# One product for the recurrence's diagonal and its lowest level

## The chip, the cores and the metric

The kernel runs on one core of a Trainium2 chip. The metric is the device time of one execution in microseconds, as the median of several runs. TensorE multiplies matrices and writes PSUM, VectorE (DVE in the profile) and ScalarE (ACT) work element by element, GpSimd (POOL) fills and copies in SBUF, and SyncE (SP) issues the loads.

## The reference, cut to what matters

The program is a two-layer trunk over 256 tokens of width 1024. Each layer is a half SwiGLU, a mixer, and another half SwiGLU. The change is in the mixer of layer 0, a gated linear recurrence (HGRN2) with 6 heads of dimension 128, beside a memory attention:

```
f = lb + (1 - lb) * sigmoid(f_raw);  q = silu(q_raw);  k = 1 - f;  v = i_raw
S_t = diag(f_t) S_{t-1} + k_t v_t^T        # per head, S is 128 x 128
o_t = S_t^T q_t
main = rms_norm(o, hgrn_o_gain) * silu(g_raw)
```

Written as scores, `o_t = sum over s <= t of (q_t * f_{s+1} ... f_t * k_s) v_s`. The score of a token with itself is `q_t . k_t`, the diagonal.

## The kernel before, in words

All data has features on the 128 partitions and tokens along the free dimension. The dense products (projections, SwiGLU) stream their weights in pieces of 128x1024 through SBUF. Each piece is split into two fp32r parts, `wh` by a cast on ScalarE (L367) and `wl` by a subtraction on VectorE (L368), and each product is taken as three fp32r matmuls.

The recurrence is computed as scores between tokens, by levels. For a block size m of 64, 32, 16, 8, 4, 2 and 1 (`LEVELS`), the tokens lie in pairs of neighbouring blocks of m. A level covers the scores of the upper block's queries with the lower block's keys. Heads go in three pairs (`hg` = 0, 1, 2), so a pair of heads has 4 tiles of 128 tokens by 128 tokens (j = 0 to 3).

`running(hg)` prepares the operands from the lowest level up. For each level, ScalarE copies the lower blocks' k into a slot of a "hid" tile (L971) and VectorE writes f times q for the upper blocks beside it (L972). Two further VectorE operations carry the running products of f to the next level, in place in `ks` and `f` (L976, L979).

`scores(hg)` does the products, in fp32. First comes the diagonal: 4 products of k with q, of 128 columns each, into one "lb" bank of PSUM, which VectorE multiplies by the identity into the score tile `s` (L1000). Then the levels come in pairs, 64/32, 16/8, 4/2, and 1 alone. Each has 4 products of 64 moving columns (the queries of the upper blocks), and a masked copy puts each level into `s` (L1017, `copy_predicated`). At last the cross product between the two tiles of each head is taken, two products, copied by ScalarE (L1024). After each bank the function pauses for a time of the planner (`DELAY["s0"]` and so on, 0.72 to 0.8 us), and dense matmuls stand in between.

The order on TensorE is fixed by a planner, `Flow`: chains such as `recurrence`, `hgrn_out`, `mem_attention` and `normed_T` are generators with due times, and after each three dense matmuls `flow.tick()` lets one due chain go on. The planner's clock runs by a cost per matmul (in `mm`) and the pauses in `DELAY`. Other engines' instructions are put in order by the framework.

Buffers that matter: "lb" has 2 PSUM banks, "mm" 3, "tb" 2, "ob" 1. "b6" has 8 SBUF buffers of 128x1560; in this mixer they hold f, kT, q, ks, i, g and a passing sq. "hid" has 11. A wait of the planner, `has("b6")`, holds a chunk until a buffer is free. The diff's `free("b6", 5)` returns the recurrence's buffers.

The mixer's projections run as chunks in the order "MMfqfqmfqigigig" (f, q, i and g of the recurrence; m and M of the memory attention), with the recurrence's products between them.

Of the kernel before, what the change touches and what calls it, by code (L numbers as in the profile page):

```python
# [15 lines left out]
ALU = mybir.AluOpType  # L16
AX = mybir.AxisListType

P = 128
T = 256  # L20
# [7 lines left out]
LEVELS = (64, 32, 16, 8, 4, 2, 1)  # L28
# [209 lines left out]
def trunk(ctx: ExitStack, tc: tile.TileContext, d: dict, out: bass.AP):  # L238
    nc = tc.nc
    V, S, G = nc.vector, nc.scalar, nc.gpsimd  # L240
# [11 lines left out]
    def bank(tag):  # L252
        return ps.tile([P, 512], F32, tag=tag, name=tag, bufs=room[tag])

    def take(tag):
        assert live[tag] < room[tag], tag
        live[tag] += 1

    def free(tag, n=1):
        live[tag] -= n  # L260
        freed[tag] = flow.now
# [7 lines left out]
    def hid():  # L269
        take("hid")  # L270
        return sb.tile([P, 4 * T], F32, tag="hid", name="hid", bufs=room["hid"])

    def b6(dt=F32):
        take("b6")
        return sb.tile([P, 1560], dt, tag="b6", name="b6", bufs=room["b6"])
# [4 lines left out]
    def unit():  # L280
        return sb.tile([P, 6 * P], F32, tag="unit", name="unit", bufs=3)
# [5 lines left out]
    def split_tiles():  # L287
        h = sb.tile([P, KT, T], F32R, tag="xh", name="xh", bufs=2)
        l = sb.tile([P, KT, T], F32R, tag="xl", name="xl", bufs=2)
        return h, l  # L290


    def mm(out, lhsT, rhs, start, stop):
        n = int(np.prod(rhs.shape[1:]))
        passes = 4 if rhs.dtype == F32 or n < 256 else 1
        flow.now += max(passes * n / 2400, 0.054) + 0.002
        nc.tensor.matmul(out=out, lhsT=lhsT, rhs=rhs, start=start, stop=stop, skip_group_check=True)  # L297
# [61 lines left out]
    def parts():  # L359
        wh = sb.tile([P, PIECE], F32R, tag="wh", name="wh", bufs=NBUF)  # L360
        wl = sb.tile([P, PIECE], F32R, tag="wl", name="wl", bufs=NBUF)
        ready.append((wh, wl))
        return wh, wl
# [16 lines left out]
    def take_piece():  # L380
        used[0] += 1
        return ready.pop(0)
# [49 lines left out]
    ident = sb.tile([P, P], F32, tag="ident", name="ident")  # L432
# [400 lines left out]
    x = split_tiles()  # L833
# [23 lines left out]
    for i in range(4):  # L857
        w = take_piece()
# [4 lines left out]
        w = parts()  # L863
# [13 lines left out]
    masks = sb.tile([P, len(LEVELS), 64], U8, tag="masks", name="masks")  # L877
# [52 lines left out]
    f, kT = b6(), b6()  # L930
# [18 lines left out]
    box = {}  # L949

    def slot(hg, i):

        return es[hg][i // 2][:, (i % 2) * 512:(i % 2 + 1) * 512]

    def halves(ap, m):
        v = ap.rearrange("p (n w m) -> p n w m", w=2, m=m)
        return v[:, :, 0, :], v[:, :, 1, :]

    def running(hg):


        es[hg] = [hid() for _ in range(4)]
        sl = slice(hg * 512, (hg + 1) * 512)
        fp, ks, k, q = f[:, sl], box["ks"][:, sl], kT[:, sl], qT[:, sl]
        for i in reversed(range(len(LEVELS))):
            m = LEVELS[i]
            n = 256 // m
            src = k if m == 1 else ks
            (f0, f1), (s0, s1) = halves(fp, m), halves(src, m)
            e0, e1 = halves(slot(hg, i), m)  # L970
            S.copy(out=e0, in_=s0)  # L971
            V.tensor_tensor(out=e1, in0=f1, in1=halves(q, m)[1], op=ALU.mult)  # L972
            low, up = f0[:, :, m - 1:m].broadcast_to([P, n, m]), f1[:, :, m - 1:m].broadcast_to([P, n, m])
            if m < 64:
                k0, k1 = halves(ks, m)
                V.tensor_tensor(out=k0, in0=s0, in1=up, op=ALU.mult)  # L976
                if m == 1:
                    S.copy(out=k1, in_=s1)
                V.tensor_tensor(out=f1, in0=f1, in1=low, op=ALU.mult)  # L979
            else:  # L980

                x = slot(hg, 7).rearrange("p (h t w m) -> p h t w m", h=2, t=2, w=2)
                h4 = lambda ap: ap.rearrange("p (h t) m -> p h t m", h=2)
                f0, f1, s0, s1, e1, q0, q1 = map(h4, (f0, f1, s0, s1, e1, *halves(q, m)))
                one = lambda ap, t: ap[:, :, t, 63:64].broadcast_to([P, 2, 64])
                V.tensor_tensor(out=x[:, :, 0, 0, :], in0=s0[:, :, 0, :], in1=one(f1, 0), op=ALU.mult)
                S.copy(out=x[:, :, 0, 1, :], in_=s1[:, :, 0, :])
                V.tensor_tensor(out=x[:, :, 1, 0, :], in0=f0[:, :, 1, :], in1=q0[:, :, 1, :], op=ALU.mult)
                V.tensor_tensor(out=x[:, :, 1, 1, :], in0=e1[:, :, 1, :], in1=one(f0, 1), op=ALU.mult)
            yield DELAY["lv"]  # L990

    def scores(hg):
        s = unit().rearrange("p (j c) -> p j c", j=6)
        ss[hg] = s
        b = bank("lb").rearrange("p (j c) -> p j c", j=4)
        for j in range(4):
            h, tt = 2 * hg + j // 2, j % 2
            sl = slice(h * T + tt * P, h * T + (tt + 1) * P)
            mm(b[:, j, :], kT[:, sl], qT[:, sl], j == 0, True)
        V.tensor_tensor(out=s[:, 0:4, :], in0=b, in1=ident.unsqueeze(1).broadcast_to([P, 4, P]), op=ALU.mult)  # L1000
        yield DELAY["s%d" % hg]
        for i0 in range(0, len(LEVELS), 2):
            b = bank("lb").rearrange("p (a j c) -> p a j c", a=2, j=4)
            pair = range(i0, min(i0 + 2, len(LEVELS)))
            for i in reversed(pair):
                m = LEVELS[i]
                for j in range(4):
                    e = slot(hg, i)[:, j * P:(j + 1) * P]
                    rows = P - m if m >= 16 else P
                    mm(b[0:rows, i - i0, j, :], e[:, 0:rows],  # L1010
                       e.rearrange("p (n w m) -> p n w m", w=2, m=m)[:, :, 1, :], i == pair[-1] and j == 0, True)
            for i in pair:
                m = LEVELS[i]
                rows = P - m if m >= 16 else P
                sv = s[0:rows, 0:4, :].rearrange("p j (n w m) -> p j n w m", w=2, m=m)[:, :, :, 1, :]
                mk = masks[0:rows, i, :].rearrange("p (n m) -> p n m", m=m)
                V.copy_predicated(out=sv, mask=mk.unsqueeze(1).broadcast_to([rows, 4, 64 // m, m]),  # L1017
                                  data=b[0:rows, i - i0].rearrange("p j (n m) -> p j n m", m=m))
            yield DELAY["s%d" % hg]
        b = bank("lb")  # L1020
        for hh in range(2):
            e = slot(hg, 7)[:, hh * T:(hh + 1) * T]
            mm(b[:, hh * P:(hh + 1) * P], e[:, 0:P], e[:, P:T], hh == 0, True)
        S.copy(out=s[:, 4:6, :], in_=b[:, 0:2 * P].rearrange("p (j c) -> p j c", j=2))  # L1024
        free("hid", 4)
        got["s"].add(hg)

    def recurrence(hg):
        yield lambda: hg in got["q"] and len(fc) > hg and fc[hg].done and (hg == 0 or hg - 1 in got["x"])
        yield lambda: live["hid"] + 4 <= room["hid"]  # L1030
        if hg == 0:
            take_ks()
        yield from running(hg)
        got["x"].add(hg)
        yield DELAY["x"]
        yield from scores(hg)
        if hg == 2:
            free("b6", 4)

    def take_ks():  # L1040
        box["ks"] = b6()

    def hgrn_out(hg):
        yield lambda: hg in got["s"] and hg in got["v"] and (hg == 2 or hg in got["g"])
# [40 lines left out]
    for hg in range(3):  # L1085
        flow.spawn(recurrence(hg), prio=PRIO["rec"])
    hc = [flow.spawn(hgrn_out(hg), prio=PRIO["hc"]) for hg in range(3)]
    mixed, mem_c, tiles = [], [], {}
    qT = None
# [243 lines left out]
```

## Time and profile before

| what | value |
|---|---|
| time before, median of 3 runs | 1061.81 us (1061.71 to 1062.89) |
| the profiled execution's own time | 1061.96 us |
| its span | 1060.2 us |
| TensorE busy | 1048.8 us (99%) |
| VectorE busy | 723.8 us (68%) |
| ScalarE busy | 533.7 us (50%) |
| GpSimd busy | 80.0 us (8%) |

The span is the time from the first to the last instruction. Busy shares are means over the whole program. Mixer A of layer 0, where the change lies, runs from about 205 to 345 us. PE is TensorE's matmuls, PEld its weight loads, which run beside them.

### The profile page before, as it was taken

How to read it: one execution, taken by the hardware profiler on the slowest of the kernel's cores; microseconds unless marked ns; L12 is line 12 of the kernel's file. 1: busy time of each engine (PE TensorE's matmuls, PEld its weight loads, DVE VectorE, ACT ScalarE, POOL GpSimd, SP SyncE). 2: the span in 40 equal slices, each digit the busy share in tenths (PEclk: the TensorE clock that was granted, in tenths of full speed). 3: DMA queues.
4: the chain of work that ended last, by engine and by line, in shares of the span. 5: the costliest groups of instructions: out<-in, count | busy, mean ns of one | idle time of the engine just before them, and what ended most of it. 6: DMA issues, size and time to landing. Idle time of an engine off the chain costs nothing.

```text
span 1060.2 us, 21472 instructions
## 1 busy us (share of the span) xinstructions
PE 1048.8 (99%) x8834; PEld 1042.8 (98%) x8834; DVE 723.8 (68%) x1331; ACT 533.7 (50%) x816; POOL 80.0 (8%) x107
## 2 busy tenths in 40 slices
PE   9899999999999999999999999999999999999998
PEld 9899999999999999999999999999999999999998
DVE  6866667689956776666687766666776577666652
ACT  7654545455544454444446544444477346445431
POOL 1000002110010500001110000012100040000000
PEclk9999999999999999999999999999999999999999
DMA  9566555553323465555553755555533245555561
GB/s 352 192 204 224 204 194 180 188 176 134 122 99 120 163 209 186 182 196 180 186 172 122 234 184 195 184 189 189 176 123 120 100 160 183 192 182 188 196 195 60
DMA packets 52874, 186.42 MB, mean 176 GB/s; under 512 B 6288, under 2 KB 7720, under 8 KB 52776
## 3 DMA queue, kind: packets, MB, share of 16 engines
q1 hardware_dynamic: 52776, 185.05, 51.3%
q8 instruction: 69, 1.13, 0.4%
q14 instruction: 29, 0.24, 0.1%
HBM read 183.95 MB, written 1.05 MB: 175 GB/s over the span
## 4 chain that ended last, share of the span: by engine, by line
PE 93%; DVE 3%; ACT 2%; DMA 2%; issue 0%; POOL 0%; SPq 0%; DVEq 0%; ACTq 0%
PE mm L297 63%; PE lb L297 26%; PE ob L297 2%; PE tb L301 1%; DMA xT<-in_xT 1%; DVE wl L368 1%; DMA b<-in_first 1%; PE tb L297 0%; ACT wh L367 0%; ACT hid L680 0%; POOL ss L481 0%; SPq L423 0%; ACT hid L487 0%; DVE small L451 0%; DVE small L453 0%
## 5 line engine op out<-in xcount | busy, mean ns | idle before, releaser
L368 DVE TENSOR_TENSOR wl<-raw,wh 128x1024 fp32r<-128x1024 f32 (+1 forms) x338 | 417.5, 1236 | 187.5 <-ACT wh L367 186.2
L367 ACT CAST wh<-raw 128x1024 fp32r<-128x1024 f32 (+1 forms) x338 | 350.8, 1039 | 297.3 <-PE mm L297 155.0
L297 PE MATMUL mm<-xh,wh 128*128 128x256 f32 x928 | 261.4, 282 | 0.0
L297 PE MATMUL mm<-xh,wl 128*128 128x256 f32 x928 | 259.1, 279 | 0.0
L297 PE MATMUL mm<-xl,wh 128*128 128x256 f32 x928 | 259.0, 279 | 0.0
L297 PE MATMUL mm<-hid,wh 128*128 128x256 f32 x1408 | 250.1, 281 | 0.0
L297 PEld LDWEIGHTS mm<-hid,wh 128*128 128x128 f32 x1408 | 216.0, 188 | 0.0
L297 PE MATMUL lb<-xh,wh 128*128 128x256 f32 x704 | 198.4, 282 | 1.6 <-ACT wh L367 1.6
L297 PE MATMUL lb<-xh,wl 128*128 128x256 f32 x704 | 197.4, 280 | 1.5 <-DVE wl L368 1.5
L297 PE MATMUL mm<-hid,wl 128*128 128x256 f32 x704 | 197.8, 281 | 0.0
L297 PE MATMUL lb<-xl,wh 128*128 128x256 f32 x704 | 197.2, 280 | 0.0
L297 PEld LDWEIGHTS mm<-xh,wh 128*128 128x128 f32 x928 | 174.5, 188 | 0.1
L297 PEld LDWEIGHTS mm<-xl,wh 128*128 128x128 f32 x928 | 174.5, 188 | 0.1
L297 PEld LDWEIGHTS mm<-xh,wl 128*128 128x128 f32 x928 | 174.4, 188 | 0.0
L297 PEld LDWEIGHTS lb<-xh,wh 128*128 128x128 f32 x704 | 133.0, 189 | 1.8 <-ACT wh L367 1.8
L297 PEld LDWEIGHTS lb<-xh,wl 128*128 128x128 f32 x704 | 133.0, 189 | 1.7 <-DVE wl L368 1.7
L297 PEld LDWEIGHTS lb<-xl,wh 128*128 128x128 f32 x704 | 133.2, 189 | 0.1
L297 PEld LDWEIGHTS mm<-hid,wl 128*128 128x128 f32 x704 | 132.6, 188 | 0.0
L297 PE MATMUL mm<-wh,xh 128*128 128x256 f32 x384 | 116.9, 304 | 0.0
L297 PE MATMUL mm<-wl,xh 128*128 128x256 f32 x384 | 108.2, 282 | 0.0
L297 PE MATMUL mm<-wh,xl 128*128 128x256 f32 x384 | 107.9, 281 | 0.0
L551 ACT CAST hid<-tmp 128x256 fp32r<-128x256 f32 x88 | 35.5, 406 | 93.9 <-DVE tmp L550 93.9
(177 smaller groups left out, 1013.2 us busy)
## 6 DMA issues: line engine op xcount, KB each, us to landing
raw<-in_wts SPq DMA_DIRECT2D x335, 512.0 KB, 3.3
b<-in_first SPq DMA_DIRECT2D x8, 384.0 KB, 6.6
hid<-in_rows SPq DMA_DIRECT2D x4, 512.0 KB
xT<-in_xT SPq DMA_DIRECT2D x2, 512.0 KB, 10.6
b<-in_memT SPq DMA_DIRECT2D x2, 512.0 KB
out_xT<-xT SPq DMA_DIRECT2D x8, 128.0 KB, 2.1
hid<-in_wts SPq DMA_DIRECT2D x1, 512.0 KB
b<-in_masks SPq DMA_DIRECT2D x1, 224.0 KB
```

The lines of the kernel that those rows point to most:

```text
L297: nc.tensor.matmul(out=out, lhsT=lhsT, rhs=rhs, start=start, stop=stop, skip_group_check=True)
L301: nc.tensor.transpose(out=out, in_=in_, identity=ident)
L367: S.copy(out=wh, in_=raw)
L368: return V.tensor_tensor(out=wl, in0=raw, in1=wh.bitcast(F32), op=ALU.subtract).ins
L551: S.copy(out=hv[:, i, :].bitcast(F32R), in_=a)
```

## The change

The lowest level and the diagonal share their weights, k: at the level of single tokens the lower block is one token and its k carries no decay yet. The new tile `near` holds, for each pair of heads and each of the 4 tiles, q for all 128 tokens and beside it f times q for the 64 odd tokens, 192 columns. One product of k with these 192 columns gives both. ScalarE copies the whole q into it (instead of the lower blocks' k into a slot), and VectorE writes f times q beside it.

In `scores`, the 4 diagonal products of 128 columns and the 4 level products of 64 become 4 products of 192, two to a bank, so in two banks. The multiplication with the identity and the masked copy of the lowest level are now done for each bank, with half the elements. The levels that are left are three pairs, and the pause after the last single level is gone. `near` takes one more buffer of "b6", beside `ks`, and is returned with it.

```
+    def near(hg):
+        return box["near"][:, hg % 2 * 768:(hg % 2 + 1) * 768].rearrange("p (j c) -> p j c", j=4)
...
-            e0, e1 = halves(slot(hg, i), m)
-            S.copy(out=e0, in_=s0)
-            V.tensor_tensor(out=e1, in0=f1, in1=halves(q, m)[1], op=ALU.mult)
+            if m == 1:
+                x = near(hg)
+                S.copy(out=x[:, :, 0:P], in_=q.rearrange("p (j t) -> p j t", j=4))
+                r4 = lambda ap: ap.rearrange("p (j n) m -> p j n m", j=4)
+                V.tensor_tensor(out=x[:, :, P:].unsqueeze(3), in0=r4(f1), in1=r4(halves(q, m)[1]), op=ALU.mult)
+            else:
+                e0, e1 = halves(slot(hg, i), m)
+                S.copy(out=e0, in_=s0)
+                V.tensor_tensor(out=e1, in0=f1, in1=halves(q, m)[1], op=ALU.mult)
...
-        b = bank("lb").rearrange("p (j c) -> p j c", j=4)
-        for j in range(4):
-            h, tt = 2 * hg + j // 2, j % 2
-            sl = slice(h * T + tt * P, h * T + (tt + 1) * P)
-            mm(b[:, j, :], kT[:, sl], qT[:, sl], j == 0, True)
-        V.tensor_tensor(out=s[:, 0:4, :], in0=b, in1=ident.unsqueeze(1).broadcast_to([P, 4, P]), op=ALU.mult)
+        one = len(LEVELS) - 1
+        mk1 = masks[:, one, :].unsqueeze(1).broadcast_to([P, 2, 64])
+        for jj in (0, 2):
+            b = bank("lb")[:, 0:384].rearrange("p (j c) -> p j c", j=2)
+            for j in range(2):
+                c = 2 * hg * T + (jj + j) * P
+                mm(b[:, j, :], kT[:, c:c + P], near(hg)[:, jj + j, :], j == 0, True)
+            V.tensor_tensor(out=s[:, jj:jj + 2, :], in0=b[:, :, 0:P], in1=ident.unsqueeze(1).broadcast_to([P, 2, P]), op=ALU.mult)
+            V.copy_predicated(out=s[:, jj:jj + 2, :].rearrange("p j (n w) -> p j n w", w=2)[:, :, :, 1], mask=mk1, data=b[:, :, P:])
         yield DELAY["s%d" % hg]
-        for i0 in range(0, len(LEVELS), 2):
+        for i0 in range(0, one, 2):
...
-            free("b6", 4)
+            free("b6", 5)
     def take_ks():
-        box["ks"] = b6()
+        box["ks"], box["near"] = b6(), b6()
```

## Rows read from the trace of the kernel before

**Rows 1.** The page: busy time of the engines, and the granted clock by slices.
```profile
PE 1048.8 (99%) x8834; PEld 1042.8 (98%) x8834; DVE 723.8 (68%) x1331; ACT 533.7 (50%) x816; POOL 80.0 (8%) x107
...
PEclk9999999999999999999999999999999999999999
```

**Rows 2.** Busy time by stretch; columns PE, PEld, DVE, ACT, POOL, clock, DMA.
```profile
235.00:265.00 30.00, 30.00 (x265) 29.87 (x264) 29.89 (x78) 16.35 (x28) 1.38 (x1) 1.00 0.40 141
265.00:295.00 30.00, 29.65 (x252) 28.98 (x250) 26.92 (x58) 18.51 (x36) 4.07 (x3) 1.00 0.38 125
295.00:325.00 30.00, 30.00 (x265) 29.76 (x264) 16.53 (x39) 11.91 (x31) 1.40 (x1) 1.00 0.25 89
```

**Rows 3.** TensorE's waits, whole span: total, times, longest; the two in mixer A.
```profile
PE tb L301 <- DVE hid L1073: 1.2, 1, 1.2
...
PE lb L297 <- DVE unit L1017: 0.4, 1, 0.4
```

**Rows 4.** Timeline of weight loads; start, length of group, engine, operation, count.
```profile
253.67 0.98 PEld L297 LDWEIGHTS lb<-b,b 128*128 128x128 f32 x8
254.57 0.19 PEld L297 LDWEIGHTS mm<-xh,wh 128*128 128x128 f32 x1
...
263.71 0.97 PEld L297 LDWEIGHTS lb<-hid 128*128 128x128 f32 x8
...
264.61 0.19 PEld L297 LDWEIGHTS mm<-xh,wh 128*128 128x128 f32 x1
...
272.88 0.98 PEld L297 LDWEIGHTS lb<-b,b 128*128 128x128 f32 x8
```

**Rows 5.** The chain that ended last, 253 to 288 us: start, length, what.
```profile
253.95 0.89 PE lb L297 x8
254.84 1.07 PE mm L297 x9
...
263.99 0.84 PE lb L297 x8
...
282.61 1.14 DVE wl L368
...
284.75 0.65 DVE unit L1017
...
285.53 0.68 PE lb L297 x4
...
287.28 0.86 PE lb L297 x4
```

**Rows 6.** Timeline of VectorE at the first and second pair of heads.
```profile
255.48 0.68 DVE L1000 TENSOR_TENSOR unit<-lb,ident 128x512 f32<-128x512 f32 x1
...
274.17 0.42 DVE L976 TENSOR_TENSOR b<-b,b 128x256 f32<-128x256 f32 x1
274.50 0.42 DVE L972 TENSOR_TENSOR hid<-b,b 128x256 f32<-128x256 f32 x1
274.84 0.69 DVE L1000 TENSOR_TENSOR unit<-lb,ident 128x512 f32<-128x512 f32 x1
275.44 0.42 DVE L979 TENSOR_TENSOR b<-b 128x256 f32<-128x256 f32 x1
```

**Rows 7.** Timeline of VectorE, 285 to 291 us.
```profile
285.55 0.72 DVE L1017 COPY_PREDICATED unit<-masks,lb 128x256 f32<-128x256 uint8 x1
286.06 0.45 DVE L979 TENSOR_TENSOR b<-b 128x256 f32<-128x256 f32 x1
...
290.85 0.28 DVE L988 TENSOR_TENSOR hid<-b,b 128x128 f32<-128x128 f32 x1
291.05 0.28 DVE L989 TENSOR_TENSOR hid<-hid,b 128x128 f32<-128x128 f32 x1
```

**Rows 8.** ScalarE copies: duration min/median/max in ns.
```profile
L971 ACT COPY hid<-b x21: 400/407/438, 233.0 to 288.4; 128x256 f32<-128x256 f32 x21
...
L690 ACT COPY hid<-tb x8: 562/586/608, 293.2 to 806.9; 128x512 f32<-128x512 f32 x8
```

More of the change, by code (lines that the diff above doesn't have):

```diff
@@ L994, in scores @@
         ss[hg] = s
-        b = bank("lb").rearrange("p (j c) -> p j c", j=4)
-        for j in range(4):
-            h, tt = 2 * hg + j // 2, j % 2
-            sl = slice(h * T + tt * P, h * T + (tt + 1) * P)
-            mm(b[:, j, :], kT[:, sl], qT[:, sl], j == 0, True)
-        V.tensor_tensor(out=s[:, 0:4, :], in0=b, in1=ident.unsqueeze(1).broadcast_to([P, 4, P]), op=ALU.mult)
+        one = len(LEVELS) - 1
[7 more added lines that the diff above has]
+            V.copy_predicated(out=s[:, jj:jj + 2, :].rearrange("p j (n w) -> p j n w", w=2)[:, :, :, 1], mask=mk1, data=b[:, :, P:])
         yield DELAY["s%d" % hg]
-        for i0 in range(0, len(LEVELS), 2):
+        for i0 in range(0, one, 2):
             b = bank("lb").rearrange("p (a j c) -> p a j c", a=2, j=4)
-            pair = range(i0, min(i0 + 2, len(LEVELS)))
+            pair = range(i0, i0 + 2)
             for i in reversed(pair):
```

## Prediction

> **What bounds the kernel now.** I read four views in turn: busy time of the engines, TensorE's list of waits, the chain of waits through the recurrence, and the timeline around the two products that are joined. The first two name the bound; the last two price the change.
>
> TensorE is busy for 1048.8 of 1060.2 us, VectorE 68% and ScalarE 50% of the span; the granted clock is full, 2.4 GHz, from start to end [rows 1]. In the stretches that hold the recurrence's products, TensorE has 30.00 and 29.65 of 30 us [rows 2]. So time removed from TensorE there is time removed from the kernel, as long as nothing makes it wait. VectorE is nearly as full: 29.89 of 30 us from 235 to 265 us [rows 2]. That is where a new wait could come from. The waits that TensorE has in mixer A are two: 0.4 us on the masked copies of L1017, and 1.2 us on L1073 at the mixer's end [rows 3].
>
> **TensorE's part.** For each pair of heads the change removes four products of 128 columns (the diagonal) and four of 64 (the level of single tokens), with the same k as weights for the diagonal. It adds four of 192. Each fp32 product stands in the trace as two weight loads and two matmuls, so four products are x8.
>
> Read the first load of a block against the first load of the next block. The diagonal takes 253.67 to 254.57, 0.90 us. The lowest level, with half the columns, takes 263.71 to 264.61, also 0.90 us [rows 4]. The chain gives 0.89 and 0.84 for the same two blocks [rows 5]. So below 128 columns a record costs the same 0.112 us (0.90 / 8): half of the lowest level's streaming time buys nothing, and that is what joining can save.
>
> No row shows 192 columns. The lower bound is proportion to columns, 8 x 0.112 x 1.5 = 1.34 us. The upper bound is the price of 256 columns, in the memory attention's logits: 0.86 us for four records, 0.215 each [rows 5], so 8 x 0.215 = 1.72 us. Two points, 0.112 at 128 and 0.215 at 256, put 192 midway at 0.164; four products are 8 x 0.164 = 1.31 us. I take that, since the middle of two measured lengths is nearer than either end. Removed 1.80, added 1.31: 0.49 us per pair of heads, and there are three pairs: **1.47 us**. With the dear end it is 3 x 0.08 = 0.24 us; with the lower chain prices (0.89 + 0.84 = 1.73) it is 1.26 us. I go on with 1.4 us.
>
> **VectorE's part.** The product with the identity, 128x512, becomes two of 128x256. From start to start the first costs 0.60 us (274.84 to 275.44), and a 128x256 operation 0.33 to 0.34 (274.17 to 274.50 to 274.84) [rows 6]. That is 2 x 0.335 - 0.60 = 0.07 us more. The lowest level's masked copy of 256 elements takes 0.51 us, from 285.55 to 286.06 [rows 7]. It becomes two of 128. They cost 0.20 each if they go as the plain 128x128 operations (290.85 to 291.05) [rows 7], and 0.51 each if half the elements save nothing; with a fixed 0.07 as in the products, 0.07 + 0.44 / 2 = 0.29. So 0.58 for 0.51. The sum is about 0.15 us per pair, 0.45 in all (bounds -0.04 to 0.6 per pair). The multiplication f1 x q of the lowest level only writes to another place. From 295 us VectorE falls to 16.53 of 30 us [rows 2], so this load is worked off there; what it costs is not the busy time but whether it arrives late for TensorE, below.
>
> A 128x256 operation lasts 0.42 us and the next starts 0.33 us after it, 0.09 us before its end [rows 6]. The Trainium skill ("VectorE: DVE Perf Modes", section "The DRAIN you can't avoid") says the next operation does not start until the pipe is empty, and asks for few operations. By that rule each operation would cost its whole duration, some 0.08 us more, and with two of them ahead of each of two waits the forecast would be some 0.3 us later, 1060.9 instead of 1060.6. The rows here show overlap, so the sum goes by them.
>
> **ScalarE's part.** The copy of the lowest level's k (128x256, 0.407 us) becomes a copy of the whole q (128x512; the nearest, out of PSUM, takes 0.586) [rows 8]: 0.18 us more, three times. It reads q instead of k, so it waits until q is final. For the first pair, levels run from 233 us and the products begin at 253.67, so the copy has well over 10 us; its cover is ScalarE's idle half. Behind it in ScalarE's order stand weight casts, whose pieces are loaded ahead; TensorE has no wait on a cast or a split in mixer A [rows 3], so I cost this at nothing, at most 0.6 us if that cover were gone.
>
> **The new buffer.** "near" takes one of eight b6 buffers for as long as ks. Live at once are f, kT, q, ks, near, i and g, seven, with the passing sq eight. The tiles that come later (FoX keys) get theirs later; only a GpSimd memset for layer 1 waits for that. No DMA and no queue is moved. I cost it at nothing; if i or g were held up until f is free, TensorE would still have another "mm" bank to fill.
>
> **Where a wait goes.** Two "lb" banks alternate. Today the order is diagonal A, levels 64/32 B, 16/8 A, 4/2 B, 1 A, cross B. The cross product waits for the 4/2 copies: VectorE passes through a weight split (282.61 in the chain), ends the second copy at 285.40, and TensorE starts at 285.53 [rows 5], 0.4 us late [rows 3]. After the change it is product pair A, product pair B, 64/32 A, 16/8 B, 4/2 A, cross B: the cross product needs a bank freed long before. But the next user of the bank of 4/2 is the memory attention's logits, which move up by the removed pause; I count half of this wait as gone, 0.2 us.
>
> The new narrow place is 64/32, which needs the first bank's product and masked copy done. For the second pair of heads TensorE starts the block at 272.88 [rows 4]; two new halves of 0.66 us and nine dense matmuls (1.07 in the chain) [rows 5] bring it to 64/32 at 275.3. VectorE starts the identity product at 274.84 behind three others [rows 6]; 0.34 + 0.29 later the bank is free, plus the last operation's tail of 0.09: 275.55. Wait 0.3 us. For the first pair the same sum is 253.67 + 1.32 + 1.07 = 256.05 against 255.48 [rows 6] + 0.72 = 256.2: wait 0.15. For the third VectorE stands idle when the diagonal is done and dense work and another head's products lie between: no wait. Together 0.45 us, less if the first half's earlier end lets VectorE start sooner.
>
> **Sum:** -1.4 - 0.2 + 0.45 = -1.15 us, rounded to -1.2. The profiled execution took 1061.96 us (span 1060.2, 1.76 around it), the median of the runs shown is 1061.81, so its own time gives 1060.8 and the median 1060.6. I predict 1060.6 us. A difference of 0.2%, 2.1 us, is what a measurement of this kernel can tell from no change: 1059.7 to 1063.9 is "same".
>
> **Rivals.**
> *More falls away than the products* (0.2): both present waits go (0.4 and 1.2 us) since the scores end one pause earlier and the order behind them shifts, and no new one comes: -1.4 - 1.6 = -3.0, 1058.8 us. For it: both waits hang on VectorE's order. Against it: the 1.2 us comes after the last pair's output product, whose place the last gate chunk sets, and that does not move.
>
> *A weight split gets ahead of the masked copy* (0.16): the bank of the first half then comes free a split later, 1.14 us in the chain [rows 5], for each pair. At all three pairs that is +3.4 on top of the 0.45: 1060.6 + 3.4 = 1064.0, slower by 0.2%. For it: just that order made today's wait, and VectorE is full up to 290 us. Against it: at the third pair VectorE is idle. With two pairs it is 1062.9, still "same". This decides for slower from about 3.3 us of new waits on.
>
> *The long product brings nothing* (0.1): 192 columns cost as 256. Gain 0.24, waits 0.25 net: 1061.8 us. For it: no row of 192. Against it: 128 and 256 are proportional.
>
> *Loads are not hidden* (0.02): then a record would cost load plus stream. From 0.112 and 0.215, 128 columns stream in 0.103 and a load adds 0.009; 64 columns would cost 0.061 and the lowest level 0.49 us instead of 0.90. The gain would be 0.90 + 0.49 - 1.31 = 0.08 per pair, 0.24 in all, 1061.8 us with the waits. The equal 0.90 of both blocks speaks against it [rows 4]. The Trainium skill ("TensorE: Matmul & The Clock Gate", section "Part 3: Packing small matmuls — row/col tiling") has such a rule: a load overlaps running matmuls only where they use other row groups. By that rule, too, nothing could be saved by hiding a load; the rows here don't agree with it.
>
> **Chances.** The forecast holds 0.52 (its own range 1059.7 to 1061.6). Faster by over 0.2%: 0.2. Slower by over 0.2%: 0.16, since later moves of the order can add to the waits. Same: the rest, 0.64. The range that leaves out no more than 2 in 10 runs from the first rival, 1058.8, to the second, 1064.0.
>
> **What would show it.** In the profile after: one block x8 of 192 columns for each pair of heads at about 0.164 us per record from load to load, none of 64 for single tokens, TensorE's matmul count lower by 24; a wait of TensorE on the masked copy before 64/32 at the second pair, and none before the cross product there; VectorE some 0.5 us busier between 235 and 310 us. The prediction is wrong if a record of 192 columns costs 0.2 us, if the wait on the masked copies exceeds 2 us in sum, or if TensorE waits for a weight split in mixer A, where it has no such wait now.

## The result, and the profile after

The change made the kernel slower: 1067.51 us (median of 6 runs, 1067.24 to 1069.33) against 1061.99 us before (6 runs), a ratio of 1.0054 with a 95% interval of 1.0044 to 1.0064. That is 5.5 us more, where 1.2 us less had been forecast, and above the forecast's range (1058.8 to 1064.0). Two executions among the experiments, 3651 us (VectorE's part alone) and 4074 us (both remedies), lie far from all others of their kernels and are left out; they were the profiled ones, so these two runs have times but no timeline to read.

The first part of the page after the change, to be laid beside [rows 1]:

```profile
span 1066.5 us, 21432 instructions
## 1 busy us (share of the span) xinstructions
PE 1049.7 (98%) x8810; PEld 1042.8 (98%) x8810; DVE 724.9 (68%) x1337; ACT 534.1 (50%) x816; POOL 80.0 (7%) x107
```

TensorE has 24 matmul records fewer, as the edit says (8810 against 8834). VectorE has 1.1 us more and ScalarE 0.4 us more over the whole span. So no engine became much busier, and the span still grew by 6.3 us. (In this pair of executions 0.8 us of the difference lies ahead of 254 us, where nothing was changed.) Most of the added time must be waiting. This is the list of TensorE's waits after the change, its longest rows; of before, [rows 3] are the two in mixer A:

```profile
PE lb L297 <- ACT wh L367: 2.1, 1, 2.1
PE ob L297 <- DVE hid L1087: 1.8, 1, 1.8
PE tb L301 <- DVE hid L1087: 1.5, 1, 1.5
PE lb L297 <- DVE wl L368: 1.4, 1, 1.4
PE lb L411 <- DVE tmp L408: 1.2, 1, 1.2
PE tb L301 <- ACT hid L684: 1.0, 1, 1.0
PE lb L297 <- DVE small L451: 0.9, 1, 0.9
PE lb L297 <- DVE unit L1014: 0.7, 1, 0.7
```

Four of them are new: on L1087 before the product into "ob" (1.8), on the exponential of the memory attention (L684, 1.0), and two before "lb" products (0.9 and 0.7). The one before the cross product (0.4) is gone. Now where they stand. This is the busy time by stretches of 10 us after the change (columns as in [rows 2], the granted clock third from the end):

```profile
250.00:260.00 10.00, 9.07 (x78) 8.76 (x77) 10.00 (x33) 5.56 (x10) 0.00 (x0) 1.00 0.32 109
...
270.00:280.00 10.00, 9.28 (x81) 8.98 (x79) 9.35 (x24) 5.57 (x11) 1.38 (x1) 1.00 0.33 118
...
290.00:300.00 10.00, 8.91 (x64) 8.04 (x63) 7.50 (x15) 8.39 (x18) 4.26 (x4) 1.00 0.33 107
...
310.00:320.00 10.00, 8.25 (x59) 8.04 (x58) 4.66 (x16) 2.15 (x4) 0.00 (x0) 0.83 0.17 56
```

Four holes, and in the last the clock is below full too. Each has one wait of 0.7 us or more in it, as the timeline of TensorE shows; the last row is the wait at the mixer's end, which the kernel before has too:

```profile
258.03 1.47 PE L297 MATMUL lb<-hid 128*96 128x64 f32 x16 [0.93 <-DVE small L451]
...
277.36 1.47 PE L297 MATMUL lb<-hid 128*96 128x64 f32 x16 [0.72 <-DVE unit L1014]
...
291.75 0.80 PE L301 MATMUL tb<-ident,hid 128*128 128x128 f32 x4 [1.00 <-ACT hid L684]
...
313.15 2.00 PE L297 MATMUL ob<-mkv,hid 128*128 128x65 f32 x16 [1.75 <-DVE hid L1087]
...
345.90 1.01 PE L301 MATMUL tb<-ident,hid 128*128 128x128 f32 x4 [1.46 <-DVE hid L1087]
```

Matmul ends are modelled, so a busy TensorE hides some waiting. From the first weight load of a block to the first load of the next, next to nothing is hidden. I read the stretches of both timelines that way, and set each against what the same number of dense matmuls takes elsewhere (0.1175 us each):

| stretch, load to load | before | after | change |
|---|---|---|---|
| diagonal and single tokens, one pair of heads | 0.90 + 0.90 | 1.25 (254.46 to 255.71) | -0.55, three times: -1.65 |
| nine dense matmuls ahead of 64/32, first pair | 1.06 | 2.29 (255.71 to 258.00) | +1.23 |
| the same, second pair | 1.07 | 2.06 (275.27 to 277.33) | +0.99 |
| third pair: joined product, and three dense ahead of 64/32 | none late | 1.61 for 1.25, 0.74 for 0.35 | +0.75 |
| nine dense ahead of the first memory transposes | 1.18 | 2.44 (289.31 to 291.75) | +1.26 |
| three dense ahead of the memory pairs' product | 0.36 (21 dense in 2.48) | 2.38 (310.76 to 313.14) | +2.02 |
| 24 dense matmuls behind that product | 2.82 (24 x 0.1175) | 4.37 (314.93 to 319.30) | +1.55 |
| nine dense ahead of the second pair's cross product | 1.65 | 1.06 | -0.59 |
| 45 dense ahead of the last transposes | 6.79 | 6.96 | +0.17 |
| sum | | | +5.73 |

From the first diagonal to the last transposes of the mixer the kernel before takes 85.85 us (253.67 to 339.52), the changed one 91.41 (254.46 to 345.87): +5.56. The table accounts for it to 0.2 us. There are two groups: 2.97 us where TensorE waits for the banks of the joined product, and 4.83 us (1.26 + 2.02 + 1.55) around the memory attention, 35 to 65 us behind the first joined product.

One reading has to be put right before it is used. The loads run one ahead of the matmuls, so the end of a joined block shows behind the first dense load. That is the second dense load, after the change and before it:

```profile
255.88 0.19 PEld L297 LDWEIGHTS mm<-xl,wh 128*128 128x128 f32 x1
...
254.68 0.19 PEld L297 LDWEIGHTS mm<-xl,wh 128*128 128x128 f32 x1
```

It comes 0.17 us after the first (255.71) behind the joined product, and 0.11 us after it (254.57) behind the diagonal. So the block takes 1.30 us and not 1.25, 0.163 for a record, which is also the spacing of the loads inside it. The joined product saves 0.50 us for each pair of heads, 1.5 in all, and some 0.1 of the 2.97 us is its tail: the bank waits are 2.9 us.

**The bank.** VectorE at the first pair of heads after the change, to be laid beside the first of [rows 6]:

```profile
256.64 0.42 DVE L1013 TENSOR_TENSOR unit<-lb,ident 128x256 f32<-128x256 f32 x1
256.97 0.17 DVE L448 TENSOR_SCALAR small<-small 128x8 int32<-128x8 int32 x1
257.04 0.42 DVE L990 TENSOR_TENSOR b<-b 128x256 f32<-128x256 f32 x1
257.38 0.17 DVE L449 TENSOR_SCALAR small<-small 128x8 int32<-128x8 int32 x1
257.45 0.44 DVE L1014 COPY_PREDICATED unit<-masks,lb 128x128 f32<-128x128 uint8 x1
257.68 0.21 DVE L451 SCALAR_TENSOR_TENSOR small<-small 128x8 f32<-128x8 f32 x1
257.73 0.42 DVE L1013 TENSOR_TENSOR unit<-lb,ident 128x256 f32<-128x256 f32 x1
```

The masked copy that frees the first bank does not follow the identity product, as the prediction had it. Three operations of other chains stand between them, and it starts 0.81 us after the product, not 0.34. The product itself comes 2.18 us after the block's first load (254.46); before the change it was 1.81 (253.67 to 255.48). The copy ends at 257.89, and TensorE goes on at 258.03, 0.14 us later. (The wait is put down to L451, which ends at the same time; the bank's reader is L1014.) The masked copy itself is cheap: 0.23 us from start to start.

**The output product.** In program order 57 dense matmuls stand between the recurrence's first output product and the memory pairs' before the change, 16.5 us (295.65 to 312.17). After it there are 24, 10.1 us (303.04 to 313.14). The loads of the two products before the change, and the first of them after:

```profile
295.65 1.43 PEld L297 LDWEIGHTS ob<-b,unit 128*128 128x128 f32 x12
312.17 1.87 PEld L297 LDWEIGHTS ob<-mkv,hid 128*128 128x128 f32 x16
...
303.04 1.42 PEld L297 LDWEIGHTS ob<-b,unit 128*128 128x128 f32 x12
```

Both products write the one "ob" bank, and the first is read by a chain of small VectorE operations that ends with four on L1087:

```profile
310.98 0.16 DVE L453 SCALAR_TENSOR_TENSOR small<-small 128x4 f32<-128x4 f32 x1
...
311.77 0.16 DVE L1081 TENSOR_TENSOR small<-small,r 128x4 f32<-128x4 f32 x1
311.96 1.13 DVE L1087 SCALAR_TENSOR_TENSOR hid<-ob,small,b 128x128 f32<-128x128 f32 x4
313.14 1.86 PEld L297 LDWEIGHTS ob<-mkv,hid 128*128 128x128 f32 x16 [1.96 <-DVE hid L1087]
```

That chain is no slower than before: it ends 10.05 us after the first output product's first load, and 9.99 us before the change (295.65 to 305.64). TensorE's order comes to the bank too early. And the clock falls behind it, in the same columns:

```profile
313.15:315.15 2.00, 2.00 (x17) 2.00 (x18) 0.00 (x0) 0.00 (x0) 0.00 (x0) 1.00 0.00 0
315.15:319.50 4.35, 4.35 (x25) 4.35 (x25) 1.83 (x3) 1.77 (x3) 0.00 (x0) 0.61 0.00 0
319.50:322.00 2.50, 2.50 (x25) 2.50 (x24) 0.75 (x1) 1.62 (x2) 0.00 (x0) 1.00 0.58 210
```

**The exponential.** The 1.00 us ahead of the memory transposes is ScalarE's order. A weight cast (L367) stands ahead of the first exponential. ScalarE is idle for 2.34 us ahead of the cast, until dense products are done; then come the cast and the load of the function's table:

```profile
288.86 1.05 ACT L367 CAST wh<-raw 128x1024 fp32r<-128x1024 f32 x1 [2.34 <-PE mm L297]
...
289.93 1.28 ACT L684 ACT_TABLE_LOAD   x1
...
291.22 0.84 ACT L684 ACTIVATE hid<-lb,small 128x256 f32<-128x256 f32 x2
```

From the logits' first load (286.63) to the exponential it takes 4.59 us. Before the change the cast there does not wait, and it takes 3.27 us (287.00 to 290.27).

### The profile page after: what moved, and what is told of

It is laid out like the page before. It is cut to its first block, busy times and chain, and to the rows that moved or that the text cites. A ratio compares the mean times of both kernels' runs of the same rounds, so it can differ in the third digit from the quotient of the medians.

```text
span 1066.5 us, 21432 instructions
## 1 busy us (share of the span) xinstructions
PE 1049.7 (98%) x8810; PEld 1042.8 (98%) x8810; DVE 724.9 (68%) x1337; ACT 534.1 (50%) x816; POOL 80.0 (7%) x107
## 4 chain that ended last, share of the span: by engine, by line
PE 89%; DVE 5%; ACT 2%; DMA 2%; issue 1%; POOL 0%; SPq 0%; DVEq 0%; ACTq 0%
PE mm L297 61%; PE lb L297 25%; PE ob L297 2%; DVE wl L368 1%; PE tb L301 1%; DMA xT<-in_xT 1%; ACT wh L367 1%; DMA b<-in_first 1%; PE tb L297 0%; ACT hid L680 0%; POOL ss L481 0%; DVE b L990 0%; DVE b L987 0%; DVE hid L983 0%; SPq L423 0%
## 5 line engine op out<-in xcount | busy, mean ns | idle before, releaser
L367 ACT CAST wh<-raw 128x1024 fp32r<-128x1024 f32 (+1 forms) x338 | 350.7, 1039 | 301.3 <-PE mm L297 159.3
```

Source lines behind the costliest of these rows:

```text
L367: S.copy(out=wh, in_=raw)
```

## The experiments

Two theories of the loss are held against each other throughout. One says that there are two causes: the bank waits, and the order of the blocks, which moved because `scores` now ends one pause of the planner earlier. Its rivals are each of the two alone, and the added work of VectorE and ScalarE. Each run was measured beside the kernel before, whose median moved by up to 0.4 us (1061.99 to 1062.35). So two runs are compared by their distances from it; the changed kernel's is 5.5 us. Most intervals are about 1 us wide on either side.

**VectorE's part alone, in the kernel before.**

```
-        V.tensor_tensor(out=s[:, 0:4, :], in0=b, in1=ident.unsqueeze(1).broadcast_to([P, 4, P]), op=ALU.mult)
+        for jj in (0, 2):
+            V.tensor_tensor(out=s[:, jj:jj + 2, :], in0=b[:, jj:jj + 2, :], in1=ident.unsqueeze(1).broadcast_to([P, 2, P]), op=ALU.mult)
...
-                V.copy_predicated(out=sv, mask=..., data=...)
+                for jj in (0, 2) if m == 1 else (None,):
+                    c = slice(0, 4) if jj is None else slice(jj, jj + 2)
+                    V.copy_predicated(out=sv[:, c], mask=..., data=...)
```

> The kernel before with VectorE's part of the change alone: the identity product and the masked copy of the lowest level are each taken in two halves. Products, banks and order stay. Theory: VectorE has 0.5 us more in all, and nothing waits for it: 1062.0 us, within 0.6. Rival, VectorE's added work is what costs: 1064 us or more, with waits at 64/32 or behind.

Measured 1061.96 us against 1062.35, ratio 0.9998 (0.9989 to 1.0007): no change. The split operations by themselves cost nothing that can be seen, within 0.9 us.

**The order alone, in the kernel before.** The pause between the levels 4/2 and 1 is taken out; products and banks stay.

```
-            yield DELAY["s%d" % hg]
+            if i0 != 4:
+                yield DELAY["s%d" % hg]
```

> The kernel before with the pause between the levels 4/2 and 1 taken out; products, banks and VectorE's work are those of before, TensorE's order of blocks is that of the changed kernel (24 dense matmuls between the first output product and the memory pairs'). Theory: the order alone brings the wait on the exponential (1.0 us), the wait at the memory pairs' product (1.7 us) and the low clock behind it (1.6 us): 1066 us. Rival, the joined product is needed for the loss: 1062 us.

Measured 1065.11 us against 1062.34, ratio 1.0024 (1.0014 to 1.0034): 2.8 us slower, without any joined product. The two waits are there, in TensorE's timeline:

```profile
289.73 0.80 PE L301 MATMUL tb<-ident,hid 128*128 128x128 f32 x4 [1.00 <-ACT hid L684]
...
310.65 2.00 PE L297 MATMUL ob<-mkv,hid 128*128 128x65 f32 x16 [1.49 <-DVE hid L1074]
```

There is no wait at 64/32. The cast stands ahead of the exponential as in the changed kernel (286.85, after 2.35 us of waiting). The low clock that was expected did not come: it stays full from 310 to 320 us, with a wait of 1.49 instead of 1.75 us.

```profile
310.00:320.00 10.00, 9.35 (x81) 9.35 (x82) 4.41 (x10) 3.79 (x6) 0.00 (x0) 1.00 0.15 53
```

Without the 1.6 us of low clock the expected time is 1064.4 us; the run came out 0.7 above that.

**The pause put back at the end of the scores.**

```
+        yield DELAY["s%d" % hg]
         b = bank("lb")
         for hh in range(2):
```

> The changed kernel with the removed pause put back ahead of the cross product. TensorE's order behind the scores is then as in the kernel before (57 dense matmuls between the first recurrence output and the memory pairs' product). Theory, two causes: the wait at the memory pairs' product, the wait on the exponential and the low clock go, the waits of 64/32 on the first bank stay (1.6 to 1.8 us), the joined product saves 1.3: 1062.5 us, within 0.7 of the kernel before. Rival, bank waits alone: 1067 us. Rival, VectorE's and ScalarE's added work: 1066 us or more.

Measured 1062.88 us against 1062.35, ratio 1.0006 (0.9997 to 1.0014). One line brings back 5.0 of the 5.5 us, with the bank waits still in place:

```profile
256.90 1.47 PE L297 MATMUL lb<-hid 128*96 128x64 f32 x16 [0.94 <-DVE small L451]
...
276.21 1.47 PE L297 MATMUL lb<-hid 128*96 128x64 f32 x16 [0.38 <-DVE unit L1014]
...
295.21 0.92 PE L297 MATMUL lb<-b,b 128*128 128x192 f32 x4 [0.46 <-ACT hid L684]
```

The third row is the second half of the third pair's product: its "lb" bank still holds the logits of a memory head. What the joined product saves is lost in these three. (In this order 60 dense matmuls stand between the two output products, three more than before the change; the wait at "ob" and the one on the exponential are gone.)

**The pause between the two halves** (as many pauses as before, and a stretch of dense work ahead of the second half).

```
             V.copy_predicated(out=s[:, jj:jj + 2, :]..., mask=mk1, data=b[:, :, P:])
-        yield DELAY["s%d" % hg]
+            yield DELAY["s%d" % hg]
```

> The changed kernel with the planner's pause put between the two halves of the joined product (two pauses instead of one, so as many as before). Theory, two causes: the 64/32 levels wait for the first bank (0.93 and 0.72 us in the changed kernel), and the memory pairs' output product comes 24 dense matmuls after the first recurrence output and waits for its bank (1.75 us, and the clock falls behind it). This edit removes the first cause only, since the output product still comes 24 dense matmuls after: 1065.7 us, with no wait at 64/32 and a wait of 1 to 2 us at the memory pairs' product. Rival, bank waits alone explain the loss: 1061 us. Rival, VectorE's and ScalarE's added work explains it: 1067 us.

Measured 1065.12 us against 1062.35, ratio 1.0029 (1.0019 to 1.0039). The time is near the expected one, but not for the reason given. The waits on the joined product's banks did not go: 1.04 us at 64/32 of the second pair, and 0.83 us at 16/8 of the first, which takes the second half's bank. The wait on the exponential is gone instead: TensorE's order from the cross product to the transposes is that of the changed kernel, but ScalarE has the cast behind it by then (286.23) and loads the table at 287.57. The wait at "ob" is 1.15 us, and the clock stays full. So this run does not separate the two causes.

**Only the memory pairs' output products later**, in the changed kernel.

```
-        yield DELAY["copy_o"]
+        yield DELAY["copy_o"] + (4.0 if l == 0 else 0.0)
```

> The changed kernel with the memory pairs' output products told to come 4.0 us later by the planner's clock: 57 dense matmuls after the recurrence's first output product, as in the kernel before, instead of 24. All else as changed. Theory: the wait of 1.75 us and the 1.6 us of low clock behind it go, the bank waits and the wait on the exponential stay: 1064.2 us, clock full behind 310 us. Rival, the low clock has another cause than this wait: 1065.8 us.

Measured 1064.53 us against 1062.34, ratio 1.0021 (1.0012 to 1.003): 2.2 us above the kernel before, so 3.3 of the 5.5 us are gone. The wait at "ob" is gone and the clock is full from 310 to 320 us; the other waits stand as they were (0.94, 0.72, 1.00, 0.15):

```profile
310.00:320.00 10.00, 10.00 (x88) 10.00 (x87) 6.22 (x18) 4.76 (x8) 0.00 (x0) 1.00 0.38 132
```

**Another bank, the order as changed.** The second half goes to a bank of "tb" (two banks, for transposes), so 64/32 finds an "lb" bank that is free.

```
-            b = bank("lb")[:, 0:384].rearrange("p (j c) -> p j c", j=2)
+            b = bank("tb" if jj else "lb")[:, 0:384].rearrange("p (j c) -> p j c", j=2)
```

> The changed kernel with the second half of the joined product in a bank of "tb", planner's pauses and TensorE's order as changed. Theory, two causes: only the waits at 64/32 go (0.93 + 0.72 + 0.3 us), the wait on the exponential, the one at the memory pairs' product and the low clock stay: 1065.7 us. Rival, bank waits alone: 1061.5 us. Rival, order alone: 1067.5 us.

Measured 1065.81 us against 1062.34, ratio 1.0029 (1.0017 to 1.0042): 3.5 us above the kernel before, so 2.1 of the 5.5 us are gone. All waits on the joined product's banks are gone, so the bank was what 64/32 waited for. They were 2.9 us. In the profiled execution the low clock takes part of that back: it lasts longer than in the changed kernel's,

```profile
310.00:320.00 10.00, 10.00 (x62) 10.00 (x62) 2.75 (x6) 3.39 (x5) 0.00 (x0) 0.66 0.15 52
```

with 24 dense matmuls in 5.10 us instead of 4.37 and the product ahead of them, 16 records, in 2.64 instead of 1.79 us: 1.6 us more.

**Both remedies at once**, the bank of "tb" and the later memory pairs (the two edits above together).

> The changed kernel with the second half of the joined product in a bank of "tb" and the memory pairs' output products 4.0 us later by the planner's clock; the pause ahead of the cross product stays out. Theory, the causes add up: 3.0 us of waits on the two banks and 3.6 us at the memory pairs' product with the low clock behind it are gone, the wait on the exponential (1.3 us) stays: 1061.5 us, within 0.7. Rival, there is a third cause of a microsecond or more: 1063 us or more.

Measured 1062.22 us against 1062.19, ratio 1.0001 (0.9992 to 1.001): the whole 5.5 us are gone, and the time is at the upper edge of what was expected. Each remedy alone took 2.1 and 3.3 us, so the causes add up. The wait on the exponential was left in by the edit; this run has no timeline that shows it. Whether that wait is all that keeps the time from falling below the kernel before was not followed.

**The products apart, in the changed kernel.**

```
-                mm(b[:, j, :], kT[:, c:c + P], near(hg)[:, jj + j, :], j == 0, True)
+                mm(b[:, j, 0:P], kT[:, c:c + P], near(hg)[:, jj + j, 0:P], j == 0, True)
+                mm(b[:, j, P:], kT[:, c:c + P], near(hg)[:, jj + j, P:], False, True)
```

> The changed kernel with each product of 192 columns taken as one of 128 and one of 64 into the same bank, all else and the planner's order the same. Every theory expects 0.22 us per product block of four... of which two blocks of two make a pair of heads: 1.80 instead of 1.31 us per pair from load to load. Theory, the saved time is lost again in the waits behind it: 64/32 of the first two pairs waits less by as much, so the time rises by 0.3 to 0.7 us only, 1068 us. Rival, TensorE's time counts in full: 1069 us.

Measured 1068.20 us against 1062.35, ratio 1.0058 (1.0044 to 1.0072), hardly more than the changed kernel's 1.0054. From the first product to the mixer's last transposes it takes 91.61 us (254.26 to 345.87), the changed kernel 91.41 (254.46 to 345.87), though the products apart cost 1.4 us more. The product block takes 1.78 us instead of 1.30 (254.26 to 256.04), and 64/32 waits 0.46 and 0.23 us instead of 0.93 and 0.72. So with those waits behind it, most of what the joined product saves is only waiting moved.

**The version without either cause**: the pause at the end of the scores and the second half in "tb".

```
-            b = bank("lb")[:, 0:384].rearrange("p (j c) -> p j c", j=2)
+            b = bank("tb" if jj else "lb")[:, 0:384].rearrange("p (j c) -> p j c", j=2)
...
+        yield DELAY["s%d" % hg]
         b = bank("lb")
         for hh in range(2):
```

> The changed kernel with the pause put back ahead of the cross product, and the second half of the joined product in a bank of "tb" instead of "lb", so that 64/32 goes to a bank that is free. Theory: with both causes gone what is left is the saving on TensorE, 1.3 us, and the waits that are not on the masked copies (0.46 before the third diagonal, 0.44 at the last output product): about 0.6 to 1.0 us below the kernel before, no wait of 64/32 on the masked copy. Rival, the joined product's work on VectorE or ScalarE costs by itself: not below the kernel before.

Measured 1060.64 us against 1062.34, ratio 0.9985 (0.9976 to 0.9994). It beats both kernels, the one before by 1.7 us, more than the 0.6 to 1.0 expected. It holds all of VectorE's and ScalarE's added work and the new buffer, so none of these is what made the changed kernel slower. TensorE's timeline lists two waits left in mixer A, both at its end:

```profile
329.18 1.58 PE L297 MATMUL ob<-b,unit 128*128 128x128 f32 x12 [0.44 <-DVE hid L1088]
338.12 1.01 PE L301 MATMUL tb<-ident,hid 128*128 128x128 f32 x4 [1.31 <-DVE hid L1088]
```

**The same version with the products apart**, to price the joined product where nothing waits behind it (the edit as above).

> The version with the pause ahead of the cross product and the second half in a bank of "tb" (1060.64 us), with each product of 192 columns taken as one of 128 and one of 64 into the same bank. TensorE waits for nothing there, so its time should count in full: 1.78 us instead of 1.25 for each pair of heads from load to load, 1.6 us in all, 1062.2 us, as the kernel before. Rival, the gain of that version comes from the wait that went (0.6 us before the cross product) or from the order: 1061 us or less.

Measured 1062.11 us against 1062.19, ratio 0.9997 (0.9989 to 1.0006). The joined product is worth the difference between these two versions: 1.6 us by their distances from the kernel before, and 1.25 us in the profiled executions from the first product to the mixer's last transposes (84.31 us, 253.78 to 338.09, against 85.56, 254.11 to 339.67). That is nearly the whole gain of the better one; the times alone would leave its size open by a microsecond.

## Why the prediction was wrong, point by point

**The joined product** was right. 1.31 us had been estimated for a block of 192 columns and 1.47 us saved for the three pairs; measured are 1.30 us and 1.5. These are the loads of the changed kernel, beside the first two of [rows 4]; with the tail behind them, 1.25 is 1.30:

```profile
254.46 1.28 PEld L297 LDWEIGHTS lb<-b,b 128*128 128x128 f32 x8
255.71 0.19 PEld L297 LDWEIGHTS mm<-xh,wh 128*128 128x128 f32 x1
```

That 64 moving columns cost as much as 128 is seen in the same view of the kernel before: with 128 columns of weights a record takes 0.112 us either way. The level pair 64/32 of the kernel before, with 64 moving columns throughout, shows that the weights set this: its loads of 96 columns follow each other after 0.085 us and those of 64 after 0.058.

```profile
255.83 0.51 PEld L297 LDWEIGHTS lb<-hid 128*96 128x96 f32 x5
...
256.49 0.54 PEld L297 LDWEIGHTS lb<-hid 128*64 128x64 f32 x8
```

The Trainium skill ("TensorE: Matmul & The Clock Gate", section "LDWEIGHTS (loading the stationary operand)") puts a load's time down to the columns of the weights alone; from its figure 128 columns come to an estimated 107 ns. The three spacings agree with it. The rival "the long product brings nothing" falls by the block's 1.30 us, where it needs 1.72. The rival "loads are not hidden" falls by the last run: the products taken apart cost 1.79 us for a pair of heads (254.11 to 255.90), where it needs 1.39.

**VectorE's and ScalarE's work** was right in that it costs nothing by itself (the run with VectorE's part alone, and the version without either cause, which has ScalarE's part too). ScalarE's copy was not run alone. The one wait on ScalarE that came, 1.00 us on the exponential, is there just as long in the run with the order alone, without that copy. The prediction counted weight casts on ScalarE at nothing since TensorE waits for none of them; here a cast delayed the exponential behind it. The cheap end was the true one for the masked copy, 0.23 us.

**Where a wait goes** is the step that failed, in two places.

First, in size. "0.34 + 0.29 later the bank is free" took the product and the masked copy as neighbours on VectorE; 0.45 us of waits came out. VectorE's order is mixed from several chains, and 0.81 us (first pair) and 0.67 us (second pair, 276.10 to 276.77) lie between the two starts. At the first pair the product also began 0.37 us later behind its block than the prediction took from before the change, and at both TensorE started some 0.14 us after the copy's end. For the third pair the prediction saw "no wait". But a product that wants two banks at once also has to wait for whoever holds the second, and that was a memory head. Measured are 1.23, 0.99 and 0.75 us, 2.9 in sum without the tails. About 2.5 us of it are on the masked copies, above the 2 us that the prediction itself named as a sign of being wrong. The rival with a weight split ahead of the masked copy named the right place but not what happens: no split stands between the product and the copy at any of the three pairs, other operations do.

Second, a term was missing. Of the removed pause the prediction said only that the memory attention's logits "move up", and it counted that as half a wait gone, 0.2 us; that wait went whole, 0.59 us by the table. Nothing asked which other blocks move with the logits, what they need by then, and who holds it. The run with the order alone shows that this costs 2.8 us by itself, and the run with the pause put back, 5.0 of the 5.5 us, that it was most of the loss. By the table the term that was missing is 4.83 us: 1.26 on the exponential, 2.02 at "ob" and 1.55 of low clock. The 1.2 us on L1073 at the end stayed where it was, as had been argued against the first rival; it is 1.46 us now.

**The low clock** was not foreseen. TensorE stood still for 1.75 us ahead of the memory pairs' product, after 1.0 us ahead of the transposes, and some 2 us after it started again the clock was low: 0.61 of full on the mean from 315.15 to 319.50, so for most of that stretch at 1.2 GHz. The two other profiled executions with such a wait show it too: 0.61 in the same stretch with the products apart (1.76 us), and 0.66 from 310 to 320 us with another bank (1.76 us). With the wait gone (pairs later) it stays full; with a wait of 1.49 us (order alone) or 1.15 us (pause between the halves) it stays full too. The Trainium skill ("TensorE: Matmul & The Clock Gate", section "HAM oscillation — how this bites in real kernels") says that idle gaps between bursts of matmuls bring the clock down again; these runs agree in direction. What makes the difference was not tried.

## What to carry to other kernels

Where one engine follows an order written by a planner, a pause or a step that an edit takes out is an edit to every block behind it. Follow the next two or three users of each single buffer (here the one "ob" bank) before counting it as free. A product joined from two should not ask for two banks at once where the next block needs the first of them back: with a bank from another group, and the pause put back, the same product gained 1.7 us instead of losing 5.5. And on an engine that is full, two operations that depend on each other need not follow each other; price the time between their starts from the distance that such pairs have in the trace, not from their durations.

## What the runs showed of the hardware that was not expected

A masked copy of 128 elements is 0.44 us long, and the next operation starts 0.23 us after it; for the one of 256 elements at the same level that was 0.51 us [rows 7], so two halves cost no more than the whole. A record of 192 columns takes 0.163 us, on the straight line between 128 and 256 columns (0.164), while with 64 moving columns the columns of the weights set the price: 0.112, 0.085 and 0.058 us for 128, 96 and 64 of them. And behind one wait of 1.75 us the low clock cost 1.55 us more, nearly as much as the wait.
